# A batch norm that streams 64 tiles through three buffers: one early load is queued at another moment

## The chip, the cores and the metric

The kernel runs on one core of a Trainium2 chip. The metric is the device time of one execution in microseconds; the figure for the kernel before is the median of three runs. A profile of one further execution (its *trace*) shows what each engine and each DMA queue did.

## What is computed

An inference batch norm over a tensor of 32 x 256 x 128 x 128 float32 values (537 MB in, 537 MB out):

```python
def reference(x, gamma, beta, running_mean, running_var):
    eps = 1e-5
    mean = running_mean.reshape(1, -1, 1, 1)
    var = running_var.reshape(1, -1, 1, 1)
    gamma = gamma.reshape(1, -1, 1, 1)
    beta = beta.reshape(1, -1, 1, 1)
    return gamma * (x - mean) / np.sqrt(var + eps) + beta
```

Per channel this is one multiply and one add: `out = x * scale + shift`, with `scale = gamma / sqrt(var + eps)` and `shift = beta - mean * scale`.

## The kernel before

**Tiles.** One image and one block of 128 channels make a tile of 128 partitions x 16384 float32, 64 KB per partition and 8 MB in all. There are `NT` = 64 of them, and `NBUF` = 3 buffers `t0`, `t1`, `t2`; tile i uses buffer i mod 3. A tile is loaded into its buffer, changed in place, and stored from it.

**Who does what.** SP issues all loads. VectorE does the first 14336 columns of a tile in two instructions (L129): `STEP` = 2560 columns, then the rest up to `VCOLS`. ScalarE does the last 2048 columns (L140) and issues the store (L153). The last tile is split at column 9216 (`VLAST`) instead. Before that, four small loads and a handful of small instructions make `scale_t` and `shift_t` (L106 to L125).

**What sets the order.** It is written out by hand with semaphores; each engine takes its instructions in program order.
- `loaded[s]` and `stored[s]` count the transfers into and out of buffer s (16 per transfer). `vdone` goes up by one with each VectorE instruction of a tile, so by two per tile; `adone` by one with each part of ScalarE.
- VectorE starts tile i when load i has landed.
- ScalarE does its part of tile i when VectorE has done its two parts and when **store i-1 has landed** (L164); then it issues store i. So one store is on its way at a time.
- SP queues loads 0 (in two halves, with the four small loads between them), 1 and 2 at the start without waiting for anything that VectorE does to a tile. From load 3 on there is a loop, L100 to L104, with two waits for each load: a separate wait until the store from the same buffer three tiles earlier has landed (L102), and a wait on the load itself until `vdone` has reached 2(i-1)+1 (L104). The latter means that load i-1 has landed and the first 2560 columns of tile i-1 are done. So from load 3 on one load is on its way at a time, and the next is issued one short VectorE instruction after it has landed.

For load 3 the two waits are: store 0 has landed, and VectorE's first part of tile 2 is done (`vdone` >= 5).

Loads and stores go through two DMA queues, q1 (issued by SP) and q10 (issued by ScalarE), on the same 16 DMA engines. Each row of 64 KB is one packet in the trace, so a tile is eight data packets on each engine.

Of the kernel before, what the change touches and what calls it, by code (L numbers as in the profile page):

```python
# [8 lines left out]
NBUF = 3  # L9
# [9 lines left out]
def kernel(  # L19
# [9 lines left out]
    nc = tc.nc  # L29
# [36 lines left out]
    stored = [sems[f"stored{s}"] for s in range(NBUF)]  # L66
    early, vdone, adone, fetched, vec, act = (sems[n] for n in names[2 * NBUF :])
# [18 lines left out]
    with tc.tile_critical():  # L86
        nc.sync.dma_start(out=bufs[0][:, left], in_=xr[order[0]][:, left]).then_inc(early, 16)
        zeroed = step(nc.vector.memset(rows[:], 0.0))  # L88
        for r, ap in enumerate((running_var, gamma, beta, running_mean)):
            inst = nc.sync.dma_start(out=rows[0:NE, r * C : (r + 1) * C], in_=ap.partition_broadcast(NE))  # L90
# [8 lines left out]

    for i in range(NBUF, NT):  # L100
        s, turn = i % NBUF, i // NBUF
        nc.sync.wait_ge(stored[s], 16 * turn)  # L102
        inst = nc.sync.dma_start(out=bufs[s][:], in_=xr[order[i]]).then_inc(loaded[s], 16)
        inst._wait_ge(vdone, 2 * (i - 1) + 1)  # L104

    step(nc.vector.memset(eps_t[:], eps))  # L106
    step(nc.vector.transpose(out=turned[:], in_=rows[:]), fetched, 16 * NPAR)  # L107
# [30 lines left out]
    def scalar_part(i, first):  # L138
        t, cb = bufs[i % NBUF], order[i] % NCB
        return nc.scalar.activation(  # L140
            out=t[:, first:],
            in_=t[:, first:],
            func=mybir.ActivationFunctionType.Identity,
            bias=shift_t[:, cb : cb + 1],
            scale=scale_t[:, cb : cb + 1],
        ).then_inc(adone, 1)
# [13 lines left out]
    for i in range(last):  # L160
        nc.scalar.wait_ge(vdone, 2 * (i + 1))
        inst = scalar_part(i, VCOLS)
# [40 lines left out]
```

## Time and profile before

| | |
|---|---|
| median of 3 runs | 2480.96 us (2480.79 to 2482.09) |
| the profiled execution | 2480.81 us, its span 2479.5 us |
| read and written | 536.94 and 536.87 MB, 433 GB/s over the span |
| VectorE busy | 508.7 us, 21% |
| ScalarE busy | 139.8 us, 6% |
| load, issue to landing | median 37.0 us (63 whole tiles) |
| store, issue to landing | median 36.5 us, 26.8 to 43.3 |
| ScalarE's waits for stores (L140) | 2274.5 us in total |
| VectorE's waits for loads (L129) | 1928.3 us in total |

The span is the profiled time from the first to the last instruction; the 1.3 us between it and the time of that execution lie around it. Both compute engines are idle most of the time, and the table names the transfers that they wait for. In the views below, `t<-in_x_dram` is a load and `out_dram<-t` a store (buffer numbers are left out), SPq and ACTq are the queues of SP and ScalarE, which issue them, DVE is VectorE and ACT ScalarE.

### The profile page before, as it was taken

To read this page: it belongs to the slowest core of one execution; us is meant where nothing else is said; L and a number is where in the kernel's file an instruction comes from. 1 tells how busy PE (TensorE), PEld (TensorE's weight loads), DVE (VectorE), ACT (ScalarE), POOL (GpSimd) and SP (SyncE) were. 2 spreads that over 40 slices of the span, in tenths; PEclk is the share of its full clock that TensorE was granted. 3 is DMA by queue.
4 is the path that set the end of the run, shared out by engine and by line. 5 is a ranking of instruction groups with operands and counts; after the bars stand their busy time and mean duration, and the time that the engine had idled before them with its cause. 6 is when DMAs were issued, how large, how long until landed. Compare 5 with 4: busy or idle time off the path is not lost.

```text
span 2479.5 us, 514 instructions
## 1 busy us (share of the span) xinstructions
DVE 508.7 (21%) x139; ACT 139.8 (6%) x66; POOL 0.2 (0%) x4
## 2 busy tenths in 40 slices
DVE  2122121221212212122121221212212122121220
ACT  0000000000000000000000000000000000000001
POOL 0000000000000000000000000000000000000000
DMA  9999999999999999999999999999999999999999
GB/s 412 435 438 427 437 438 429 436 438 429 435 438 430 435 439 430 433 438 433 431 438 432 432 438 432 432 438 432 432 438 433 431 438 433 431 438 435 430 438 410
DMA packets 18708, 1073.85 MB, mean 433 GB/s; under 512 B 2128, under 2 KB 2192, under 8 KB 2192
## 3 DMA queue, kind: packets, MB, share of 16 engines
q1 hardware_dynamic: 9488, 536.94, 50.1%
q10 hardware_dynamic: 9216, 536.88, 50.0%
q14 instruction: 4, 0.03, 0.0%
HBM read 536.94 MB, written 536.87 MB: 433 GB/s over the span
## 4 chain that ended last, share of the span: by engine, by line
DMA 92%; DVE 4%; another core or an unknown queue 2%; ACT 0%; issue 0%; SPq 0%; DVEq 0%
DMA t<-in_x_dram 92%; DVE t L129 4%; ACT t L140 0%; SPq L90 0%; DVE rows L88 0%; DVEq L98 0%; SPq L86 0%
## 5 line engine op out<-in xcount | busy, mean ns | idle before, releaser
L129 DVE TENSOR_SCALAR t<-t,scale_t,shift_t 128x11776 f32<-128x11776 f32 (+2 forms) x128 | 505.2, 3989 | 1928.4 <-DMA t<-in_x_dram 1928.3
L140 ACT ACTIVATE t<-t,shift_t,scale_t 128x2048 f32<-128x2048 f32 x64 | 138.2, 2159 | 2297.3 <-DMA out_dram<-t 2274.5
L107 DVE STREAM_TRANSPOSE turned<-rows 32x1024 f32<-32x1024 f32 x1 | 1.2, 1232 | 7.6 <-DMA rows<-in_running_mean_dram 7.6
L114 ACT ACT_TABLE_LOAD x1 | 1.3, 1283 | 6.4 <-PEq L98 6.4
L88 DVE MEMSET rows<- 32x1024 f32 x1 | 0.9, 912 | 1.2 <-SPq L86 1.2
L106 DVE MEMSET eps_t<- 128x1 f32 x1 | 0.1, 59 | 4.4 <-PEq L98 4.4
L114 ACT ACTIVATE std_t<-par,eps_t 128x2 f32<-128x2 f32 x1 | 0.3, 295 | 8.5 <-DVE par L112 8.5
L112 DVE COPY par<-turned 32x8 f32<-32x8 f32 x4 | 0.7, 162 | 0.1
L121 DVE RECIPROCAL rstd_t<-std_t 128x2 f32<-128x2 f32 x1 | 0.2, 165 | 0.4 <-ACT std_t L114 0.4
L122 DVE TENSOR_TENSOR scale_t<-par,rstd_t 128x2 f32<-128x2 f32 x1 | 0.2, 161 | 0.0
L123 DVE TENSOR_TENSOR ms_t<-par,scale_t 128x2 f32<-128x2 f32 x1 | 0.2, 161 | 0.0
L124 DVE TENSOR_TENSOR shift_t<-par,ms_t 128x2 f32<-128x2 f32 x1 | 0.2, 160 | 0.0
L187 POOL MEMSET const-bfloat16-1.0<- 128x1 bf16 x1 | 0.1, 101 | 0.0
L187 POOL MEMSET const-uint8-127<- 128x1 uint8 x1 | 0.1, 101 | 0.0
L187 POOL MEMSET const-float32-0.0<- 128x1 f32 x1 | 0.1, 98 | 0.2 <-issue 0.2
L187 POOL MEMSET const-float32-1.0<- 128x1 f32 x1 | 0.1, 98 | 0.0
## 6 DMA issues: line engine op xcount, KB each, us to landing
t<-in_x_dram SPq DMA_DIRECT2D x2, 4096.0 KB, 16.0
out_dram<-t ACTq DMA_DIRECT2D x64, 36.5
t<-in_x_dram SPq DMA_DIRECT2D x63, 37.0
rows<-in_running_var_dram SPq DMA_DIRECT2D x1, 16.0 KB, 11.2
rows<-in_gamma_dram SPq DMA_DIRECT2D x1, 16.0 KB, 11.0
rows<-in_beta_dram SPq DMA_DIRECT2D x1, 16.0 KB, 10.7
rows<-in_running_mean_dram SPq DMA_DIRECT2D x1, 16.0 KB, 10.7
```

Of the source, the lines that this page charges most:

```text
L88: zeroed = step(nc.vector.memset(rows[:], 0.0))
L106: step(nc.vector.memset(eps_t[:], eps))
L107: step(nc.vector.transpose(out=turned[:], in_=rows[:]), fetched, 16 * NPAR)
L112: placed = step(nc.vector.tensor_copy(out=flat[q * B : (q + 1) * B], in_=blocks[:, :, q, 0]))
L114: nc.scalar.activation(out=std_t[:], in_=var_t, func=mybir.ActivationFunctionType.Sqrt, bias=eps_t[:], scale=1.0,)._wait_ge(vec, placed).t ...
L121: step(nc.vector.reciprocal(out=rstd_t[:], in_=std_t[:]), act, 1)
L122: step(nc.vector.tensor_mul(out=scale_t[:], in0=gamma_t, in1=rstd_t[:]))
L123: step(nc.vector.tensor_mul(out=ms_t[:], in0=mean_t, in1=scale_t[:]))
L124: ready = step(nc.vector.tensor_sub(out=shift_t[:], in0=beta_t, in1=ms_t[:]))
L129: return nc.vector.tensor_scalar(out=t[:, first:end], in0=t[:, first:end], scalar1=scale_t[:, cb : cb + 1], scalar2=shift_t[:, cb : cb + 1 ...
L140: return nc.scalar.activation(out=t[:, first:], in_=t[:, first:], func=mybir.ActivationFunctionType.Identity, bias=shift_t[:, cb : cb + 1] ...
L187: nc = _bacc.Bacc("TRN2", target_bir_lowering=False, num_devices=1)
```

## The change

In the loop that issues loads 3 to 63, load 3 (i = `NBUF`) is treated apart: the separate wait (L102) is not issued for it, and its own wait is for store 0 instead of for `vdone`. All other loads keep both waits.

```diff
     for i in range(NBUF, NT):
         s, turn = i % NBUF, i // NBUF
-        nc.sync.wait_ge(stored[s], 16 * turn)
+        if i > NBUF:
+            nc.sync.wait_ge(stored[s], 16 * turn)
         inst = nc.sync.dma_start(out=bufs[s][:], in_=xr[order[i]]).then_inc(loaded[s], 16)
-        inst._wait_ge(vdone, 2 * (i - 1) + 1)
+        if i > NBUF:
+            inst._wait_ge(vdone, 2 * (i - 1) + 1)
+        else:
+            inst._wait_ge(stored[s], 16 * turn)
```

The data are safe by that one wait: load 3 overwrites `t0`, which store 0 has read when it has landed.

## The prediction

> **What bounds the kernel now.** First the page: span, busy share, bytes and queues.
>
> ```profile
> span 2479.5 us, 514 instructions
> ...
> DMA  9999999999999999999999999999999999999999
> GB/s 412 435 438 427 437 438 429 436 438 429 435 438 430 435 439 430 433 438 433 431 438 432 432 438 432 432 438 432 432 438 433 431 438 433 431 438 435 430 438 410
> ...
> q1 hardware_dynamic: 9488, 536.94, 50.1%
> q10 hardware_dynamic: 9216, 536.88, 50.0%
> ```
>
> The 16 DMA engines are busy in all 40 slices; loads (q1) and stores (q10) take half each. A store is 144 packets (9216 / 64): 128 of data, one row of 64 KB each, eight per engine, and 16 that only raise the semaphore. One data packet takes 0.500 x 16 x 2479.5 / (64 x 128) = 2.42 us; the packet records of the trace say 2.418 us, the next starting 2.414 us after. A load and a store together are 16 packets per engine, 16 x 2.414 = 38.63 us.
>
> Second, stretches of one such period (columns: stretch, its length, busy time of VectorE, ScalarE and GpSimd, clock, DMA share, GB/s), and the two ends:
>
> ```profile
> 88.80:127.38 38.58, 7.35 (x2) 2.09 (x1) 0.00 (x0) 1.00 1.00 431
> 127.40:166.01 38.61, 7.07 (x3) 2.09 (x1) 0.00 (x0) 1.00 0.98 424
> ...
> 1054.50:1093.13 38.63, 7.93 (x3) 2.09 (x1) 0.00 (x0) 1.00 1.00 434
> ```
>
> ```profile
> 0.00:2.00 2.00, 0.78 (x1) 0.00 (x0) 0.20 (x4) 1.00 0.28 82
> ...
> 2476.00:2478.00 2.00, 0.00 (x0) 0.00 (x0) 0.00 (x0) 1.00 0.23 98
> 2478.00:2480.00 2.00, 0.00 (x0) 0.00 (x0) 0.00 (x0) 1.00 0.00 0
> ```
>
> 1073.85 MB at 434 GB/s are 2474.3 us. The first window is short of 434 by 2 x (434 - 82) / 434 = 1.6 us, the last two (3.5 us up to the end of the span) by 3.5 - 2 x 98 / 434 = 3.0 us. Together 2478.9 of the 2479.5 us: all that lies between is worth some 0.6 us. The bound is the 16 engines.
>
> Third, the chain of waits and the waits of SP's queue, which name something else:
>
> ```profile
> 88.75 37.50 DMA t<-in_x_dram
> 126.25 0.03 issue
> 126.28 1.62 DVE t L129
> 127.92 37.81 DMA t<-in_x_dram
> ```
>
> ```profile
> SPq L102 <- DMA out_dram<-t: 1395.0, 61, 66.0
> SPq L103 <- DVE t L129: 984.8, 61, 16.5
> ```
>
> The chain runs load, 1.62 us of VectorE, next load; SP stands about 16 us at each load for VectorE's count. It looks as if each load came 1.66 us late (1.62 + 0.03 + the step between). But a load lasts 37 us only because store packets lie between its own; while no load is queued, the store has the engines.
>
> Last, the stretch that the change touches (columns: start, length, engine, line):
>
> ```profile
> 72.39 2.09 ACT L140 ACTIVATE t<-t,shift_t,scale_t 128x2048 f32<-128x2048 f32 x1 [43.34 <-DMA out_dram<-t]
> 74.52 0.34 ACTq L153 DMA_DIRECT2D out_dram<-t  x1
> 87.11 7.93 DVE L129 TENSOR_SCALAR t<-t,scale_t,shift_t 128x2560 f32<-128x2560 f32 x2 [23.47 <-DMA t<-in_x_dram]
> 88.75 117.60 SPq L103 DMA_DIRECT2D t<-in_x_dram  x4
> 111.40 2.09 ACT L140 ACTIVATE t<-t,shift_t,scale_t 128x2048 f32<-128x2048 f32 x1 [36.91 <-DMA out_dram<-t]
> 113.52 0.34 ACTq L153 DMA_DIRECT2D out_dram<-t  x1
> 126.28 7.93 DVE L129 TENSOR_SCALAR t<-t,scale_t,shift_t 128x2560 f32<-128x2560 f32 x2 [31.23 <-DMA t<-in_x_dram]
> ```
>
> Store 0 lands at 72.4, load 2 at 87.09; load 3 goes out at 88.75.
>
> **The change, part by part.** One of 61 loads loses its wait for VectorE; no transfer, byte or instruction of VectorE, ScalarE or GpSimd is added or dropped. The separate wait (L102) of that one load goes too, its condition moving onto the load: tens of nanoseconds on SP, which then waits some 40 us for store 1. Nothing: 0 us.
>
> *The move.* Load 3 goes out at 72.45, 16.3 us earlier, behind load 2 in the same queue. What follows I count in packets, by what the packet records show. (a) With work in both queues, an engine alternates, packet by packet, and the semaphore packet takes a turn too: between load 1's last packet (ends 49.7) and load 2's first (54.5), queued back to back, lie two store packets. (b) A transfer lands 2.72 to 2.80 us after its last data packet if the other queue has work (one packet and 0.35), 0.35 to 0.42 us after it if not (the last two stores). (c) From issue to first packet it is 3.35 to 6.33 us behind a busy other queue, 1.0 to 1.6 us on idle engines (the first load: 0.95 to 1.95 and on).
>
> Load 2's last packets end at 83.5 to 84.3, as before. Two packets of store 1 follow (4.83 us), and load 3 starts at 88.3 to 89.1, not at 93.2 to 94.0. Store 1, begun at 78.7, has then sent three; its five others alternate with load 3's eight. Load 3's last packet ends 13 x 2.414 = 31.4 us on, at 119.7 to 120.5. Store 1's ends after ten of the 13, at 112.5 to 113.3, and lands at 116.05 (before: 111.37, so 4.7 us later). ScalarE's 2.09 us and 0.06 of issue put store 2 at 118.2 (before 113.52). Load 3 lands at 120.9 with the store queue still empty, at 123.3 if a store packet is ahead of its semaphore; 1.66 us on, load 4 goes out at 122.5 to 124.9, not 127.92. Its other wait, store 1, is over at 116.05. So loads come about 5.4 us earlier, stores 4.7 later, and the engines serve the same packets in another order.
>
> *The cost of that order.* Load 3's last packet and store 2's first now meet. Store 2, out at 118.2, can be on the engines at 119.2 to 119.8, and the slowest engine runs out of load packets at 120.5: covered, by 0.7 to 1.3 us. Load 4 then starts after three store packets (120.5 + 4.83 = 125.3 is only 2.8 us after its issue, less than the 3.35; 127.7 is the next end of a packet), or after four if it landed later. From there the pattern repeats: three store packets, ten alternating, three load packets. In those three (7.24 us) a store must land (2.75), pass ScalarE and issue (2.15) and reach the engines (1.0 to 1.6): 5.9 to 6.5 us, covered by 0.7 to 1.3. The period stays 16 packets, 38.63 us. If that cover is gone, idle time comes back in each period (first rival). At the end, store 62 goes out before load 63 has landed, and store 63 some 6.4 us after it (ScalarE's last part), under store 62's 19.3 us alone: nothing idle.
>
> *The sum:* 2479.5 + 0 = 2479.5 us of span, + 1.3 around it (the profiled execution took 2480.81, the median is 2480.96). I take **2481.0 us**. What can scatter is how far the slowest engine falls behind: the packet records end at 2476.6 to 2479.0, so some 2 us either way: 2478.6 to 2483.5.
>
> The Trainium skill, "DMA: Bandwidth & Descriptors", section "Rules for kernel authors", says to issue a DMA early so that its fixed set-up cost is overlapped; the Trainium skill's section on the anatomy of one DMA, in the same page, puts that cost at about 2.0 us for GpSimd's path. Taken as time saved, it would give some 2479.0, an estimate by that page, and stands beside rival 3 below; the rows above say that the gap is covered by store packets already. The Trainium skill, the same page's "Specifications", gives a ceiling of 435 GB/s: 1073.85 MB in 2468.6 us, an estimate by it, 10.9 below the span, which leaves room for a faster result; the trace runs at 434, and its two ends leave 0.6.
>
> **The rivals.**
> 1. *Stores and loads fall into step* (slower). If load 4 came in after two store packets, not three, stores would end only two packets (4.83 us) before the loads, and 5.9 to 6.5 us of landing, ScalarE and issue would no longer be covered: 1.07 to 1.67 us idle per period. It keeps itself up, as then the next load is early again. From 120 to 2445 us there are 60 periods: 64 to 100 us, 2545 to 2581 us. It decides at a first packet less than 2.8 us after the issue, or at a store over 1.3 us later than I count. For it: a margin near 0.6 us. Against it: 3.35 is the smallest of all later loads on 16 engines.
> 2. *One idle stretch at the handover.* Should store 2 need the longest delay (118.2 + 6.33 = 124.5) after the load packets end at 120.5, up to 4.0 us go once, 6 with the scatter: 2482 to 2487. Against: those delays were seen only behind a running queue.
> 3. *The 1.66 us of the gap are saved once:* 2479.3. For it the chain of waits; against it the 0.6 us above.
> 4. *The early load carries through to the end* (faster): loads 5.4 us earlier all along, 2475.5. The chain, 92% loads, speaks for it; the full engines against.
> 5. *The change does not take effect,* because load 3 waits for something else: 2481. SP's wait for VectorE ended last there, so this is unlikely.
>
> **How the numbers follow.** Forecast 0.63, rivals 0.15, 0.12, 0.06, 0.03 and 0.01. A measurement of this kernel tells about 0.2%, 5 us: below 2476.0 is faster, above 2485.9 slower. Faster: rival 4, 0.03. Slower: rival 1 and under half of rival 2, 0.20. The rest, 0.77, is the same. The range 2477.5 to 2488 takes in all but rivals 1 and 4, 0.82; the forecast's own is 2478.6 to 2483.5.
>
> **What would show it.** Load 3 issued at 72.4 and landing near 121 (or 123); store 1 landing at 116; load 4 issued at 122.5 to 125; after that loads 38.6 us apart, and each store issued some 32 to 34 us after the load before it, where it is 24.6 now; 434 GB/s in every period. A load landing near 126 again would refute the count; a period of 39.7 or more, and DMA slices under 430, would show rival 1; a GB/s dip at 120 alone, rival 2.

## The result, and the profile after

The changed kernel takes 2592.34 us (median of five runs, 2585.27 to 2595.95), the kernel before 2480.96 us: a ratio of 1.0448, 95% interval 1.0436 to 1.0460. It is 111 us slower. The forecast of no change was wrong. The first rival came in part only: as shown below, it accounts for about half of the loss. The profiled execution took 2595.95 us, its span is 115.2 us longer than before.

The page of the changed kernel first (its lines have moved by four: L104 issues the loads, L133 is VectorE, L144 and L157 are ScalarE and its stores).

```profile
span 2594.7 us, 513 instructions
...
DMA  9999999999999999999999999999999999999999
GB/s 421 420 428 401 415 417 407 420 403 419 406 420 404 424 416 420 404 434 406 420 407 417 420 404 420 420 404 420 408 416 420 404 404 419 397 407 425 415 395 418
...
q10 hardware_dynamic: 9216, 536.88, 49.7%
q1 hardware_dynamic: 9488, 536.94, 49.3%
...
out_dram<-t ACTq DMA_DIRECT2D x64, 38.0
t<-in_x_dram SPq DMA_DIRECT2D x63, 38.7
```

Packets and bytes are the same. The DMA engines still show 9 in every slice, and yet move 395 to 428 GB/s in all but one of them; before, it was 427 to 439 in all but the first and the last. A packet that stalls counts as busy. The loss is spread over the whole run, not at the place of the change.

The stretch that was changed (columns: start, length, engine, line), and below it the chain of waits there:

```profile
72.45 253.64 SPq L104 DMA_DIRECT2D t<-in_x_dram  x7
...
115.93 2.09 ACT L144 ACTIVATE t<-t,shift_t,scale_t 128x2048 f32<-128x2048 f32 x1 [41.38 <-DMA out_dram<-t]
118.06 0.34 ACTq L157 DMA_DIRECT2D out_dram<-t  x1
120.75 7.94 DVE L133 TENSOR_SCALAR t<-t,scale_t,shift_t 128x2560 f32<-128x2560 f32 x2 [25.85 <-DMA t<-in_x_dram]
```

```profile
72.45 48.27 DMA t<-in_x_dram
120.72 0.03 issue
120.75 1.62 DVE t L133
122.37 0.02 issue
122.39 38.70 DMA t<-in_x_dram
161.09 0.03 issue
161.12 1.62 DVE t L133
162.74 0.02 issue
162.76 39.87 DMA t<-in_x_dram
```

Load 3 goes out at 72.45 and lands at 120.72 (counted: 120.9), store 1 lands at 115.9 (116.05), store 2 goes out at 118.06 (118.2), load 4 at 122.39 (122.5). So far the count of packets held within 0.2 us. From there loads take 37.6 to 40.7 us instead of 36.97, and the period from issue to issue is 39.3 to 42.4 us instead of 38.63.

Two stretches from the middle of the run show what has changed between the two queues; in each, a store goes out and then VectorE starts on the next load that has landed:

```profile
1051.30 0.34 ACTq L157 DMA_DIRECT2D out_dram<-t  x1
1052.21 7.93 DVE L133 TENSOR_SCALAR t<-t,scale_t,shift_t 128x2560 f32<-128x2560 f32 x2 [31.98 <-DMA t<-in_x_dram]
...
1091.18 0.34 ACTq L157 DMA_DIRECT2D out_dram<-t  x1
1093.84 7.93 DVE L133 TENSOR_SCALAR t<-t,scale_t,shift_t 128x2560 f32<-128x2560 f32 x2 [33.69 <-DMA t<-in_x_dram]
```

A store goes out 2.7 us (118.06 to 120.75, 1091.18 to 1093.84) or only 0.9 us (1051.30 to 1052.21) before VectorE starts on a load that has landed; the smallest value of the run is 0.3. Before, it was 12.8 us: 113.52 to 126.28. This offset is what the change has moved, and it lies between 0.3 and 2.9 us to the end.

### The profile page after: what moved, and what is told of

The parts are those of the page before. It is cut to its first block, busy times and chain, and to the rows that moved or that the text cites. A ratio compares the mean times of both kernels' runs of the same rounds, so it can differ in the third digit from the quotient of the medians.

```text
span 2594.7 us, 513 instructions
## 1 busy us (share of the span) xinstructions
DVE 508.8 (20%) x139; ACT 139.8 (5%) x66; POOL 0.2 (0%) x4
## 4 chain that ended last, share of the span: by engine, by line
DMA 94%; DVE 4%; ACT 0%; issue 0%; SPq 0%; DVEq 0%
DMA t<-in_x_dram 93%; DVE t L133 4%; DMA out_dram<-t 2%; ACT t L144 0%; SPq L90 0%; DVE rows L88 0%; DVEq L98 0%; SPq L86 0%
## 5 line engine op out<-in xcount | busy, mean ns | idle before, releaser
L133 DVE TENSOR_SCALAR t<-t,scale_t,shift_t 128x11776 f32<-128x11776 f32 (+2 forms) x128 | 505.3, 3989 | 2038.0 <-DMA t<-in_x_dram 2037.9
L144 ACT ACTIVATE t<-t,shift_t,scale_t 128x2048 f32<-128x2048 f32 x64 | 138.2, 2159 | 2407.0 <-DMA out_dram<-t 2393.7
```

The costliest lines, as they stand in the source:

```text
L133: return nc.vector.tensor_scalar(out=t[:, first:end], in0=t[:, first:end], scalar1=scale_t[:, cb : cb + 1], scalar2=shift_t[:, cb : cb + 1 ...
L144: return nc.scalar.activation(out=t[:, first:], in_=t[:, first:], func=mybir.ActivationFunctionType.Identity, bias=shift_t[:, cb : cb + 1] ...
```

## Where 115 us go: the packet records

The records name queue, start and length of each packet; packets that follow each other without a gap belong to one engine, so each engine's sequence can be read off. (Across an idle stretch the pairing is a guess; the means below do not depend on it.) One engine of the changed kernel, twice, and one of the kernel before (L a load packet, S a store packet, with the start in us; +x: longer by x than the usual 2.418):

```
after   ... L112.94 L115.36 L117.78 S120.20(+0.74) S123.35 S125.76 L128.19 S130.60 ...
after   ... L1043.48 L1045.90 L1048.31 [idle 1.5] S1052.24 S1054.68 S1057.12(+0.44) L1059.97(+1.94) S1064.32 ...
before  ... S105.56 L107.98 L110.39 L112.81 L115.22 S117.64 L120.05 S122.47 ...
```

The pattern is the one counted, three store packets, alternation, three load packets. But at the place where the load's last packet is followed by the store's first, called the *seam* here, time is lost. From the 60 seams of the changed kernel (stores 2 to 61), the mean per engine: idle before the first store packet 0.46 us, first store packet too long 0.52, later store packets 0.30, the next load's first packet 0.58, its others 0.06. Together 1.92 us, and 60 x 1.92 = 115 us, the whole of it. In the kernel before the same sum is 0.4 us over the whole run.

Starts of stores on all engines, by how old the store's issue is when the engine has finished the packet before:

| age of the issue | starts | idle, mean us | first packet too long, mean us |
|---|---|---|---|
| under 0.5 us (after) | 295 | 0.6 to 1.7 | 0.03 to 0.05 |
| 0.5 to 1 (after) | 69 | 0.10 | 0.21 |
| 1 to 2.5 (after) | 593 | 0.00 | 0.73 to 0.88 |
| 3 and over (before) | 992 | 0.00 | 0.00 |

(Left out: 19 starts after still longer idle times, and the 16 of store 1, over 4 us old and without loss. The oldest issue with a loss is 2.4 us old, the youngest without one 3.39; the runs below fill that gap.)

Two kinds of seam follow. In 39 of the 60 the store's issue is 2.3 to 2.4 us old when the slowest engine's load packets end (0.3 to 1.8 for the fastest engine), the first store packet takes some 0.8 us more, and 1.2 us are lost in all; the next load mostly comes in after three store packets or more, as forecast. In the other 21 the engines stand idle (1.28 us on the mean engine), and the packets around the next load's start take 0.71 and 1.20 us more: 3.28 us in all. (21 x 3.28 + 39 x 1.19 = 115.3.) In 17 of these 21 the store goes out late, 1.5 us or less before the slowest engine's load packets end and mostly about with it; each time some engine had let the load before in after two store packets instead of three, and there is no period with such an engine that was not followed by this. That is the condition of the first rival. These 17 seams lose 58.5 us; the other 43 lose 56.8 us, which no rival had. In the other four of the 21 the store goes out 2.3 us ahead of the slowest engine's end, but the other engines had finished before the slowest.

**Theory (lead):** what counts is the moment of a store's issue against the end of the load's packets. Issued over some 3.4 us ahead, its first packet follows without loss; later than that, each period loses, and the period is so built that the next store is late again. (The table leaves the limit anywhere between 2.4 and 3.4 us.) **Rivals:** two loads queued back to back leave something behind in the queue; or reads and writes in separate bursts (three load packets, three store packets) are slow in themselves.

## The experiments

**Load 10 once later by 6.3 us** (in the changed kernel).

```diff
-            inst._wait_ge(vdone, 2 * (i - 1) + 1)
+            inst._wait_ge(vdone, 2 * (i - 1) + (2 if i == 10 else 1))
```

> The changed kernel, with one load, load 10, made to wait for both of VectorE's parts of tile 9 instead of the first alone, so that it goes out 6.3 us later, once. Theory (lead): from load 10 on the stores go out well before the load packets end, and the period falls from about 40.5 to 38.63 us for the rest of the run; six or seven slow periods of some 1.85 us are left: 2491 to 2497 us. Rival (back-to-back loads leave something behind for good): about 2590. Rival (what is lost hangs on each transfer in this order, not on the moment): about 2590.

Measured: 2492.64 us (2484.23 to 2493.64, three runs). The windows before and after load 10, which goes out at 370.6 (columns as in the prediction):

```profile
240.00:280.00 40.00, 7.94 (x2) 2.33 (x2) 0.00 (x0) 1.00 0.96 393
400.00:438.60 38.60, 7.93 (x2) 2.09 (x1) 0.00 (x0) 1.00 1.00 435
1000.00:1038.60 38.60, 7.93 (x2) 2.09 (x1) 0.00 (x0) 1.00 1.00 435
```

One late load, and the rest of the run is at full rate again. In its packet records the stores' issues are 2.4 us or less ahead up to load 9 and 9.5 to 9.8 us ahead from load 10 on. Here, too, load 3 was queued right behind load 2; and from 1000 us on the records show mostly four or six load packets in a row and as many store packets, longer bursts than the three of the changed kernel, at 435 GB/s. Both rivals of the theory fall, and so does the last one of the expectation.

**The same shift put elsewhere:** the kernel before, with load 20 queued early instead of load 3.

```diff
-        nc.sync.wait_ge(stored[s], 16 * turn)
+        if i != 20:
+            nc.sync.wait_ge(stored[s], 16 * turn)
         inst = nc.sync.dma_start(out=bufs[s][:], in_=xr[order[i]]).then_inc(loaded[s], 16)
-        inst._wait_ge(vdone, 2 * (i - 1) + 1)
+        if i != 20:
+            inst._wait_ge(vdone, 2 * (i - 1) + 1)
+        else:
+            inst._wait_ge(stored[s], 16 * turn)
```

> The kernel before, in which load 20 instead of load 3 is queued as soon as its buffer's store has landed, behind load 19. Theory (lead): the same shift of loads against stores, only later: periods of 38.63 us up to load 20, and about 1.85 us more in each of the some 43 periods after it, 80 us: 2545 to 2575 us. Rival (the harm is in the start, where loads 0 to 3 then stand four deep): 2481 to 2483.

Measured: 2568.73 us. The page's GB/s, a slice being 64 us, so that load 20's moment (some 730 us) is in the twelfth:

```profile
GB/s 411 439 427 439 438 428 439 427 440 428 440 429 405 393 409 425 417 417 416 417 409 410 409 425 409 425 409 409 425 409 424 409 395 423 423 411 409 409 406 412
```

Full rate up to there, 393 to 425 from there to the end. The start of the kernel has no part in it.

**How large must the delay be?** Load 10 once later by 1.4 us, or by 2.9 us, by a longer first part of tile 9 (5120 or 8192 columns instead of 2560).

```diff
-        vector_part(i, 0, STEP)._wait_ge(*landed(i))
-        vector_part(i, STEP, VLAST if i == last else VCOLS)
+        cut = 5120 if i == 9 else STEP
+        vector_part(i, 0, cut)._wait_ge(*landed(i))
+        vector_part(i, cut, VLAST if i == last else VCOLS)
```

> The changed kernel, with one instruction of VectorE cut elsewhere: the first part of tile 9 has 5120 columns instead of 2560, so that load 10 goes out 1.4 us later, once. Theory (lead): the load still comes in after three store packets, the first packet boundary that it can make (about 8.1 us after the load packets end, for an issue at 3.4 and the 3.36 us that it needs at least); the stores still go out 2.34 us before the load packets end, and nothing is gained: 2580 to 2596 us. Rival (any later load helps in proportion, 1.4 us being a part of the 6.3 of the run before): some way between, 2510 to 2570.

> The same with 8192 columns: load 10 goes out 2.9 us later, once. Theory (lead): the load comes in after four store packets, from then on the stores go out about 4.75 us before the load packets end, the first store packet no longer stalls, and the period is 38.63 us to the end: 2488 to 2497 us, as with the delay of 6.3 us. Rival (in proportion): 2510 to 2550.

Measured: 2591.57 and 2494.88 us. 1.4 us buys nothing, 2.9 us buys all that 6.3 us bought. With 2.9 us, from then on:

```profile
438.19 0.34 ACTq L157 DMA_DIRECT2D out_dram<-t  x1
445.78 7.93 DVE L133 TENSOR_SCALAR t<-t,scale_t,shift_t 128x2560 f32<-128x2560 f32 x2 [31.69 <-DMA t<-in_x_dram]
```

The store goes out 7.6 us before the load lands, which is 4.8 us before the last load packet of the slowest engine ends (a landing comes 2.77 us later where store packets wait) and some 3.0 before that of the fastest. The place of one load among the packets moves in whole packets; there is no proportion.

**The early load by itself:** load 3 early, and load 4 once later by 6.3 us (the edit of the first experiment with `i == 4`).

> The changed kernel, with load 4 made to wait for both of VectorE's parts of tile 3, so that it goes out some 6.3 us later, once, right behind the early load 3. Theory (lead): the early load by itself costs one stall of 0.85 us at the handover near 120 us and gains nothing; the period is 38.63 us from then on: 2480.5 to 2484 us. Rival (back-to-back loads leave something behind): about 2590. Rival (the load that is early is worth its 5.4 us once the stores are out of its way): 2475 to 2477.

Measured: 2482.44 us (2481.31 to 2485.63, ten runs), ratio 1.0005, interval 0.9996 to 1.0015. Its records lose 2.7 us in all, the first seam among them. The early load by itself costs a few us at most and is worth nothing.

**Half of the change undone:** load 3 waits for load 2's landing, without VectorE.

```diff
-        inst._wait_ge(vdone, 2 * (i - 1) + 1)
+        if i > NBUF:
+            inst._wait_ge(vdone, 2 * (i - 1) + 1)
+        else:
+            inst._wait_ge(*(loaded[i - 1], 16))
```

> The kernel before, with load 3 going out when load 2 has landed, without VectorE's 1.62 us: 1.66 us earlier instead of 16.3. Theory (lead): load 3 starts one store packet earlier than before (about 90.8 instead of 93.2), the stores still go out some 4.75 us before the load packets end, over the 3.4 they need, and nothing stalls: 2480 to 2483 us. Rival (each us by which the load is early costs its share): 2490 to 2495 us, a tenth of 111.

Measured: 2482.83 us (2482.18 to 2483.66), ratio 1.0006, interval 0.9996 to 1.0017.

```profile
115.48 0.34 ACTq L156 DMA_DIRECT2D out_dram<-t  x1
123.08 7.94 DVE L132 TENSOR_SCALAR t<-t,scale_t,shift_t 128x2560 f32<-128x2560 f32 x2 [28.30 <-DMA t<-in_x_dram]
```

7.6 us again, and its records have load 3's first packet at 90.7 to 91.3, as counted: one packet earlier costs nothing that is clear of the noise, two cost 111 us. The starts of stores in this run and in the one with 2.9 us fill the gap of the table: 12 with an issue 2.6 to 2.8 us old took 0.54 us too long on the mean, 82 at 2.8 to 3.0 took 0.12, and 407 at 3.0 to 3.2 took 0.00. So the limit is about 2.9 us, and not the 3.4 of the theory.

**The cause doubled:** loads 3 and 4 early (`if i > NBUF + 1` in both places of the change).

> The suspected cause doubled: loads 3 AND 4 are queued as soon as their buffers' stores have landed, each behind the load before it. Theory (lead): load 4 follows load 3 without a gap, its packets and those of store 2 alternate from the start and end within one packet of each other, near 160 us; then both queues are dry, for some 3 us, until the next load and the next store come in together, and this repeats: 3 us of idle engines and 1 to 2 us of stalls in each of some 59 periods: 2650 to 2780 us. Rival (the harm is what it is once the loads are no longer paced from the start, one more makes no difference): 2585 to 2600.

Measured: 2713.15 us. The chain of waits runs along the stores now:

```profile
118.49 2.10 ACT t L144
120.59 0.02 issue
120.61 42.33 DMA out_dram<-t
162.94 0.03 issue
162.97 2.10 ACT t L144
165.07 0.02 issue
165.09 40.04 DMA out_dram<-t
```

From landing to landing a store takes 44.5 us and then 42.2, where it was 38.63. The packets of a load and a store alternate from the start and end together. Per period and engine, 2.1 us are idle time before the load's first packet, and load packets take 1.7 us too long.

**Three cures that do not bring the time back.** Later loads, by a longer first part of VectorE, and earlier stores, by a shorter part of ScalarE, for all tiles of the changed kernel:

```diff
-STEP = 2560
+STEP = 8192
```

```diff
-VCOLS = 14336
+VCOLS = 16128
```

> The changed kernel, with VectorE's first part of each tile 8192 columns long instead of 2560 (4.55 us instead of 1.62), so that every load from 4 on goes out 2.9 us LATER. Theory (lead): in the changed kernel each store goes out only 2.34 us before the load packets end on the slowest engine, and a store packet whose issue is less than some 3.4 us old at that moment costs a stall or an idle stretch. A later load comes in after four store packets instead of three, the store ends four packets before the load, and goes out 4.7 us before the load packets end: nothing stalls, the period is 38.63 us, and the time is 2481 to 2486 us. Rival (two loads queued back to back leave something behind in the queue for good): about 2590. Rival (reads and writes in separate bursts are slow in themselves): no better than 2590, since four and four packets are apart now instead of three and three.

> The changed kernel, with ScalarE's part of tiles 0 to 62 cut from 2048 to 256 columns (VCOLS 16128; about 0.6 us instead of 2.09), so that each store goes out some 1.5 us sooner after the one before it has landed; the loads are as in the changed kernel. Theory (lead): a store then goes out about 3.8 us before the load packets end, over the 3.4 us, and the stall at the store's first packet (32 us per engine over the run) and the idle stretches before it (27 us) go. If the stalls of the load's first packet (35 us) and of the store packet before it (18 us) only follow from these, 2481 to 2486 us; if they have a cause of their own, 2520 to 2540. Both rivals (back-to-back loads leave something behind; separate bursts of reads and writes): about 2590.

> The changed kernel, with ScalarE's part of tiles 0 to 62 cut from 2048 to 768 columns (VCOLS 15616; about 1.0 us instead of 2.09). With 256 columns the stores went out early enough at first, then gained on the loads period by period until the load's first packet met the end of the store's. Theory (lead): with 768 the store goes out about 3.4 us before the load packets end, just enough, and its turn (1.1 us) is only 0.5 us shorter than the load's (1.66), as much as the load's is shorter in the kernel before, where it does not show: 2481 to 2495 us. Rival (shorter turns in themselves bring the two out of step): 2550 as with 256 columns.

(The third has VCOLS 15616.) Measured: 2673.54, 2556.09 and 2515.34 us; the expected numbers failed in all three. The page of the first, slices of 67 us:

```profile
GB/s 412 435 426 439 425 400 400 398 387 408 392 398 402 392 408 392 408 392 393 408 392 408 391 393 408 391 410 392 392 408 392 408 386 399 392 407 397 389 408 392
```

For five slices it runs as forecast. What the theory says of the stores holds in all three: their first packets and the idle time before them, 59.5 us per engine in the changed kernel, come to 0.9, 0.1 and 0.2 us in the whole run. But time is lost at the other seam, from the store's last packet to the load's first. Call *turn* the time from a transfer's landing to the next issue in its queue. In the first of the three a load's turn (4.55 us of VectorE) is longer than a store's (2.1 of ScalarE), so the stores gain some 5 us per period on the loads, from load 5 to load 9, until the load comes too late for the end of the store's packets: its first packet starts mostly 0.95 to 1.9 us after its issue, on idle engines. In all, 80 us of idle time lie before the loads' first packets, and load packets take 108 us too long; the theory has no reason for the latter. With 256 and 768 columns ScalarE takes 0.60 and 1.03 us, 1.0 and 0.6 less than the 1.62 of VectorE; the stores gain on the loads as early, up to load 8 or 9, and it costs less.

Two controls tell whether the early load has a part in that: the same two sizes in the kernel before.

> A control: the kernel BEFORE with ScalarE's part cut to 256 columns. Theory (lead, and turns that must match): the early load is not what makes 2556 us of the changed kernel with 256 columns; the stores' turn of 0.65 us against the loads' 1.66 lets the stores gain on the loads until the load's first packet is issued too late before the store packets end, wherever they began: 2545 to 2565 us here as well. Rival (what is left there is a remainder of the early load's harm): 2481 to 2490.

> A control: the kernel BEFORE with VectorE's first part 8192 columns long. Theory: the loads' turn of 4.6 us against the stores' 2.15 lets the stores gain on the loads in the same way: 2660 to 2685 us, as in the changed kernel with 8192. Rival (a remainder of the early load's harm): under 2580.

Measured: 2561.79 and 2682.65 us, about what the changed kernel has with these sizes. The early load has no part in it. In all five runs in which the stores drift against the loads, the load's turn is the longer one, by 0.6 to 2.5 us. In the kernel before it is the store's, by 0.49 us (2.15 against 1.66), and its records show stores 9.5 to 10.0 us ahead from the second to the last period. Two differences of about the same size, 0.6 and 0.49 us, have opposite signs and opposite outcomes, which suggests that the sign matters and not the size alone; a store's turn longer by more than 0.49 us was not run. No version beat the kernel before.

## Why the prediction was wrong

**Right:** the bound (16 engines, 434 GB/s), the missing gain (no run is faster than before), the packets' order at the handover, and the moments of load 3, store 1, store 2 and load 4 within 0.2 us. The small margin was named, and so was the mechanism of the first rival (a load in after two store packets makes the next store late); it was given 0.15.

**The step that failed** is the cost of the new order: "the slowest engine runs out of load packets at 120.5: covered, by 0.7 to 1.3 us". The prediction had two delays from issue to first packet, 1.0 to 1.6 us on idle engines and 3.35 and more behind a busy queue, and took the first for a store that goes out 2.34 us before the load packets end, while that queue still ran. The start was covered, as said; but a first packet covered by so little is not free. The table above shows what it put at nothing: 593 such first packets follow without idle time and take 0.73 to 0.88 us too long each, while 992 whose issue was at least 3 us old lose nothing. It also counted the cover for the slowest engine alone; in four seams the others stood idle although the store was 2.3 us ahead of that one.

**From there the first rival follows,** in 17 seams of 60, but not by the signs given for it (a first load packet less than 2.8 us after its issue, or a store over 1.3 us later than counted). The 0.8 us at the store's first packet moves the end of the second store packet from 4.83 to about 5.7 us after the load packets end, 3.6 us after load 4's issue. That is over the 3.35 that the fastest engines need, so that some engine can let the load in after two; in the 17 seams it did so 3.4 to 3.7 us after the issue. One engine is enough, as a store lands with its slowest: the next store goes out up to 2.4 us later, and the engines stand idle. Each of the 17 was followed by this. Nor did it keep itself up from period to period, as the rival had it: after each such pair the load came in after three store packets again. Rivals 3 and 4, a gain of 1.66 or 5.4 us from the early load, fall with the run in which only load 3 is out of place (2482.44 us); rival 2, idle time at the first seam alone, falls too: that seam cost 0.9 us per engine, a stall without idle time, and the others followed; rival 5 falls with load 3's issue at 72.45.

**The size:** the rival was priced at 1.07 to 1.67 us per period, and the measured loss is 1.92. That the two lie close is luck: the price held idle time alone, in every period; of that there are 0.46 us on the mean, and the rest are packets that take longer. The slices of GB/s showed it, as foretold; the DMA engines' busy share did not, since a stalled packet is a busy one.

**The rule of the Trainium skill** ("DMA: Bandwidth & Descriptors", section "Rules for kernel authors"), issue early to hide the set-up cost, would have given some 2 us less, an estimate by that page's figure for GpSimd's path. The runs of this kernel do not bear it out: early by one packet or early and then late again is worth nothing (ratios of 1.0006 and 1.0005), early by two packets costs 111 us.

## What to carry to other kernels

When two queues share the engines and each is re-issued after its own landing, their offset in time is a state that one early or late transfer can set for the rest of the run. Look at the time from one queue's issue to the end of the other's packets (here about 3 us or more on every engine, for a store behind a load), not at the wait that is removed. Compare the two turns, too: in the five runs here in which the load's turn was longer than the store's by 0.6 us or more, the offset drifted to a bad place by itself. A single late transfer early in the run was enough here to set the offset right again.

## What the runs showed of the hardware

- A transfer lands 0.35 us after its last packet on an otherwise empty set of engines and 2.77 us after it where the other queue has packets: its semaphore packets wait for one packet of that queue (2.41 us).
- The extra 0.73 to 0.88 us of a store's first packet hardly shrink as its issue grows from 1 to 2.4 us old, and are gone at 3 (0.54 us at 2.6 to 2.8, 0.12 at 2.8 to 3.0). A fixed delay that is only partly covered would shrink; what makes it a step is open.
- After a seam with idle engines, the third store packet and the next load's first one take 0.7 and 1.2 us more, though the load's issue is mostly over 6 us old. Why was not found. Packets other than the store's first make up 57 of the 115 us, and some 40 of these lie here.
